# RWKV norm of a hybrid layer: scale, shift and bonus merged with the gate in the input projection, its rows reordered block by block

## The chip, the cores and the metric

The kernel runs on one core of a Trainium2 chip. The metric is the device time of one execution in microseconds. The engines of a core work side by side: TensorE (PE, with its weight loads PEld), VectorE (DVE), ScalarE (ACT), GpSimd (POOL) and SyncE (SP), which issues most DMAs.

## The reference, cut to what matters

One layer of a hybrid backbone: 2048 latent tokens and 256 context tokens, width 1024. One input projection feeds two groups of heads, a bidirectional RWKV-7 (512 wide, 8 heads of 64) and a latent attention (512 wide). Each is multiplied by its own SiLU gate; one output projection, the residual and a final norm follow.

```
u_sh, g_rw, u_mla, g_mla = split(h @ w_in)           # h: normed, modulated x
us = token_shift(u_sh, mu)                           # us + mu_prev*(prev-us) + mu_next*(next-us)
r, k, v, ... = split(us)                             # 512 channels each
y = y_f + y_b                                        # RWKV scans of both directions
yn = (y - mean) * rsqrt(var + 64e-5) * lnx_g + lnx_b # over the 64 channels of a head
bonus = sum(r * (k_dir[0] + k_dir[1]) * r_k, -1) * v # sum over a head, times v
rw_l = (yn + bonus) * silu(g_rw)
mla_l = attention(...) * silu(g_mla)
x = x + gate * (concat(rw_l, mla_l) @ w_out);  out = rms_norm(x) * final_g
```

## The kernel before, in words

**Projection.** `h` stands in SBUF with channels on the partitions, as a high and a low half. Two sweeps cover the tokens: the first 1026 latent ones with the 256 of the context, then the rest. In a sweep each *row* is a block of 128 columns of `w_in` (class `Row`): its weights are loaded into `wraw` by SP (L95, one buffer), split into `whi` on ACT and `wlo` on POOL, and multiplied with each group of tokens in 24 matmuls (L117: `whi` by high, `whi` by low, `wlo` by high, 8 each). A row has three latent groups of 342 columns (`h0`, `h1`, `h2`); rows with `ctx=True` have a fourth of 256 (`hc`) in the first sweep. ACT copies each result to `u` (four buffers). The next row's object, and with it the load of its weights, is made after the first group of the current row (`row`, L839).

Work behind a row is a generator in `self.pend`; `step` runs one step of the first of them after each sixth matmul, and `flush` runs all that are left. So the order in which rows are written sets under which rows the work of a block lies. The framework's scheduler decides the final order on each engine in this phase, from this order and from costs of its own.

**Order of rows in `sweep`.** First latent rows and the decay and rate rows, then for each of four blocks of 128 channels an `r` and a `k` row; then four `v` rows; then gate rows (six in the first sweep, eight in the second, where `ada_gate` adds two matmuls of a single row to each of the first four). After an `r`, `k` pair `flush` runs, `shift` (L848) makes the shifted `r` in `usr` (one buffer) and the shifted `k` in `us` (two buffers): one ACT pass and two DVE passes each. Then `rk_block` (L907) is queued, which lies under the next two rows: for each piece of at most 512 tokens `rk_piece` (L927) squares `k`, sums the squares over a head on PE with `blk`, a matrix with two blocks of ones (L937), multiplies decay and rate by their small weights (L954, L955), makes decays, directions and their running sums (POOL, ACT, DVE) and stores them to `s_x` (L969, L979). At its end it makes `bs = (kd0 + kd1) * r_k * r` (DVE, L988, which reads `usr`) and queues `finish`, run one piece later or by `last_bonus` (L921): four matmuls of two columns (L994) sum `bs` over each head, and DVE copies the sums to `bon`, one number for each token and head. `v_piece` (L1003) transposes the shifted `v` on PE and stores it to `s_v`, tokens on the partitions. `gate_out` (L815) makes `g = (tanh(u/2) + 1) * u / 2` and stores it to `s_g` on SP in the first sweep, on POOL or ACT in the second.

**Middle.** `qkv`, the RWKV chunks and the attention follow; PE's order there is written out by hand (`core`, L1190). An attention job takes scores in two passes: maxima first (L1307 on PE, `TENSOR_REDUCE` L1308 on DVE), then exponentials (L1427 to L1429 on PE, L1431 on ACT), accumulations on POOL (L1436) and values on PE (L1454).

**Tail.** Under the last four jobs (11 to 14 of the list) `late` (L1236) hands out, at each of its calls, a share of the steps of `post` (L1484), so that they are through after `POST_T` of the calls; the rest goes to `out_tiles`, the output projection (L1611). `post` loads the output weights, multiplies them by the gate, splits them, and then does 16 tiles of 128 tokens, three of which are under way at a time. On DVE a tile has: add of both directions (L1548), sum (L1551) and mean (L1553), subtraction (L1554), **bonus times `v`** (L1557), sum of squares (L1559, L1560), **plus shift** `lb` (L1567), times the inverse deviation (L1569), **times scale** `lg` (L1571), sum of both (L1573), product with the gate out of the transposed bank (L1582), and the low half of the split (L549). Each `yield` is one step.

## Time and profile before

| | |
|---|---|
| runs of the kernel before | median 2989.06 us, 2982.56 to 3002.37 us, 3 runs |
| the profiled execution | 3012.28 us, span of the trace 3010.5 us |
| PE (TensorE) | 2714.7 us busy, 90% of the span |
| PEld (weight loads) | 2061.7 us, 68% |
| DVE (VectorE) | 1810.0 us, 60% |
| POOL (GpSimd) | 1389.4 us, 46% |
| ACT (ScalarE) | 1285.2 us, 43% |
| HBM | 111 GB/s over the span |

Busy shares are averages over stages that have different limits, so a change is weighed in the stage in which it lies. The first stage (to about 190 us) makes the first `h`; the sweeps lie at 190 to 499 us and 641 to 946 us; `post` runs from 2428 to 2763 us; after that only output tiles and the last attention work are left. In rows of the trace "A <- B" reads "A waited for B", and a number behind an x counts instructions.

### The profile page before, as it was taken

The page shows a single profiled execution, that of the slowest core. Times are in us where ns is not written, and L with a number is a line of the kernel's source. Part 1 is how long each engine was busy: PE and PEld are TensorE (multiplying, and loading weights), DVE is VectorE, ACT ScalarE, POOL GpSimd, SP SyncE. Part 2 cuts the span into 40 slices and gives each one's busy share as a digit, 9 for nine tenths or more (in the row PEclk, how much of TensorE's full clock was granted, in tenths as well). Part 3 has the DMA queues.
Part 4 walks back from the last instruction along what each step waited for, and adds up shares of the span by engine and source line. Part 5 has one row for each costly group of instructions (what it writes and reads, how often), then busy time and mean ns, then how long its engine had stood idle before and what let it go on. Part 6 is the DMA issues. An engine that isn't in the chain of part 4 may idle for free.

```text
span 3010.5 us, 55075 instructions
## 1 busy us (share of the span) xinstructions
PE 2714.7 (90%) x22035; PEld 2061.7 (68%) x22035; DVE 1810.0 (60%) x2832; ACT 1285.2 (43%) x2245; POOL 1389.4 (46%) x1220
## 2 busy tenths in 40 slices
PE   5999999999998898999998999998999977888998
PEld 3997899987788787666666666566666644445776
DVE  3346843346623566777765777666677667997223
ACT  3446744446533432454443444444454432332221
POOL 2323322323332122566665666565566545776332
PEclk7998999999999998999998999999999977889999
DMA  5224552225554876222132222133122054343543
GB/s 200 82 87 124 136 161 92 80 92 140 149 157 160 267 224 162 75 86 70 54 103 82 61 71 69 52 101 99 58 76 61 22 153 117 110 126 108 150 134 119
DMA packets 409466, 336.66 MB, mean 112 GB/s; under 512 B 130598, under 2 KB 341841, under 8 KB 408185
## 3 DMA queue, kind: packets, MB, share of 16 engines
q1 hardware_dynamic: 405775, 327.19, 37.1%
q8 instruction: 173, 2.83, 0.4%
q0 software_dynamic: 992, 3.21, 0.3%
q10 hardware_dynamic: 2442, 2.73, 0.3%
q14 instruction: 84, 0.69, 0.1%
HBM read 210.68 MB, written 122.31 MB: 111 GB/s over the span
## 4 chain that ended last, share of the span: by engine, by line
PE 64%; DVE 15%; DMA 7%; ACT 5%; issue 4%; POOL 3%; SPq 1%; ACTq 0%; POOLq 0%; DVEq 0%
PE pm L117 18%; PE bo L1454 7%; PE bx L1611 6%; PE bs L1427 4%; DVE m L1308 3%; DMA x<-s_x 3%; PE bs L1429 3%; PE bs L1307 3%; PE bs L1428 3%; PE bx L331 3%; PE bs L1097 2%; ACT pt L1431 2%; PE bc L407 2%; DVE x L251 2%; PE bx L433 1%
## 5 line engine op out<-in xcount | busy, mean ns | idle before, releaser
L1436 POOL TENSOR_TENSOR acc<-acc,pt 128x512 f32<-128x512 f32 x512 | 662.6, 1308 | 581.3 <-ACT pt L1431 577.3
L1431 ACT ACTIVATE pt<-bs 128x512 f32<-128x512 f32 x576 | 342.7, 596 | 523.7 <-PE bs L1429 497.5
L1308 DVE TENSOR_REDUCE m<-bs 128x1 f32<-128x512 f32 (+1 forms) x736 | 400.0, 567 | 187.8 <-PE bs L1307 183.9
L1427 PE MATMUL bs<-q,kt 97*128 97x512 f32 x576 | 283.7, 493 | 46.5 <-DVE m L1308 27.9
L1454 PE MATMUL bo<-pt,vt 128*64 128x512 f32 x1152 | 301.8, 648 | 0.0
L549 POOL TENSOR_TENSOR wlo<-wraw,whi 128x1024 fp32r<-128x1024 f32 (+1 forms) x56 | 134.5, 2401 | 264.7 <-PE pm L117 163.9
L1307 PE MATMUL bs<-kt,q 96*128 96x512 f32 (+1 forms) x480 | 183.1, 410 | 71.1 <-ACT pt L1431 31.7
L1429 PE MATMUL bs<-q,kt 97*128 97x512 f32 x576 | 238.5, 414 | 0.0
L1428 PE MATMUL bs<-q,kt 97*128 97x512 f32 x576 | 238.1, 413 | 0.0
L1427 PEld LDWEIGHTS bs<-q,kt 97*128 97x128 f32 x576 | 113.5, 197 | 124.7 <-DVE m L1308 38.9
L1307 PEld LDWEIGHTS bs<-kt,q 96*128 96x128 f32 x480 | 91.5, 191 | 139.9 <-ACT pt L1431 68.2
L132 ACT COPY u<-pm 128x342 f32<-128x342 f32 (+1 forms) x168 | 73.9, 441 | 210.9 <-PE pm L117 209.5
L1454 PEld LDWEIGHTS bo<-pt,vt 128*64 128x64 f32 x1152 | 77.1, 146 | 121.1 <-issue 114.0
L1429 PEld LDWEIGHTS bs<-q,kt 97*128 97x128 f32 x576 | 114.9, 200 | 27.7
L1611 PE MATMUL bx<-wohi,big 128*128 128x512 f32 x496 | 126.0, 395 | 4.0 <-DMA big<-s_mix 4.0
L1428 PEld LDWEIGHTS bs<-q,kt 97*128 97x128 f32 x576 | 115.9, 201 | 4.8
L978 POOL TENSOR_TENSOR xt<-z,nk 128x512 f32<-128x512 f32 (+1 forms) x40 | 53.2, 1329 | 142.7 <-ACT z L977 82.0
L1611 PEld LDWEIGHTS bx<-wohi,big 128*128 128x128 f32 x496 | 93.7, 190 | 25.2 <-issue 4.9
L371 DVE TENSOR_TENSOR R<-bx,R 128x512 f16<-128x512 f32 x108 | 73.6, 682 | 59.1 <-PE bx L331 58.0
L1647 DVE TENSOR_TENSOR acc<-bx,big 128x512 f32<-128x512 f32 x32 | 22.1, 689 | 143.3 <-PE bx L1611 138.3
L826 DVE SCALAR_TENSOR_TENSOR kd<-z,u 128x512 f32<-128x512 f32 x32 | 38.9, 1218 | 111.4 <-ACT z L824 111.4
L348 DVE TENSOR_TENSOR bdg<-bx,lvl 64x512 f16<-64x512 f32 x144 | 98.6, 685 | 5.2 <-PE bx L331 2.6
(320 smaller groups left out, 6392.8 us busy)
## 6 DMA issues: line engine op xcount, KB each, us to landing
wraw<-in_w_in SPq DMA_DIRECT2D x54, 512.0 KB
x<-s_x SPq DMA_DIRECT2D x72, 384.0 KB
s_x<-xt SPq DMA_DIRECT2D x32, 512.0 KB
big<-s_mix SPq DMA_DIRECT2D x24, 512.0 KB
s_kn<-hl SPq DMA_DIRECT2D x36, 256.0 KB
ar<-s_nr SPq DMA_DIRECT2D x72, 128.0 KB
uv<-s_v SPq DMA_DIRECT2D x72, 128.0 KB
s_x<-cum SPq DMA_DIRECT2D x32, 256.0 KB
```

Source lines behind the costliest of these rows:

```text
L117: nc.tensor.matmul(ps[0:m, 0:w], a[:, k, 0:m], x[:, k], start=n == 0, stop=n == 3 * KT - 1)
L348: nc.vector.tensor_tensor(self.bd[name][ur, :, ur], x[ur], self.lvl[ur, i, ur].unsqueeze(1).to_broadcast([64, 8, 64]), op=ALU.mult)
L549: (eng_lo or nc.vector).tensor_tensor(lo, x, hi.bitcast(F32), op=ALU.subtract)
L1307: nc.tensor.matmul(ps[:, 0:w], q[0:96, e, 0, i * P:(i + 1) * P], ks[e], start=True, stop=True)
L1308: nc.vector.tensor_reduce(m5[:, e * NQS + i, j:j + 1], ps[:, 0:w], axis=AX.X, op=ALU.max)
L1427: nc.tensor.matmul(ps, ks[:, e, 0, sl], q[:, e, 0], start=True, stop=False)
L1428: nc.tensor.matmul(ps, ks[:, e, 0, sl], q[:, e, 1], start=False, stop=False)
L1429: nc.tensor.matmul(ps, ks[:, e, 1, sl], q[:, e, 0], start=False, stop=True)
L1431: nc.scalar.activation(pt, ps, AF.Exp, scale=SCALE)
L1436: nc.gpsimd.tensor_tensor(acc[e], held[e] if kt == 1 else acc[e], pt, op=ALU.add)
L1454: nc.tensor.matmul(oo[64 * e:64 * e + 64], VS[j][:, i, 64 * e:64 * e + 64], pts[kt, e], start=kt == 0, stop=kt == NK - 1)
L1611: nc.tensor.matmul(ps, x[:, i], a[:, k, 512 * h:512 * h + 512], start=n == 0, stop=n == last)
```

## The change

It does three things.

1. The rows of a sweep are ordered block by block: `v`, `r`, `k`, gate of block 0, then of block 1, and so on; the gate rows that belong to the attention come last, and `ada_gate` goes behind gate row 4. `rk_block` is queued after the `k` row and so lies under the gate row of its block and the `v` row of the next.
2. Shift, scale and bonus move into the projection, where channels are on the partitions. `bs` gets half of `r_k`; `finish` sums it with one matmul of 512 columns whose result has each head's sum on all of its 64 partitions, and multiplies the shifted `v` with it in place. The new `gate_rwkv(b)` runs after the `v` row of the next block: g = (tanh(u/2) + 1) * u, vp = (v * bonus/2 + lnx_b/2) * g, gl = g * lnx_g/2, and SP stores `vp` to the new `s_vb` and `gl` to `s_g`.
3. In the tail a tile is then y_normed (transposed) * gl + vp. The bonus product, the shift's add and the scale go; the remaining operations are spread over the steps anew. `POST_T` goes from 0.75 to 0.7, and the count of steps in `late` from 11 a tile to 7.

Cut to what matters:

```
     def sweep(...)
         for b in range(4):
-            specs += [(b * P, P, False), (512 + b * P, P, True)]
-        specs += [(1024 + b * P, P, True) for b in range(4)]
-        specs += gates[:6] if s == 0 else gates
+            specs += [(1024 + b * P, P, True), (b * P, P, False), (512 + b * P, P, True), gates[b]]
+        specs += gates[4:6] if s == 0 else gates[4:]
...
+        gg = None
         for b in range(4):
-            rr, kk = self.row(), self.row()
+            vv = self.row()
+            self.flush()
+            if b:
+                self.gate_rwkv(b - 1, gg, uv)
+            rr = self.row()
+            vs = self.shift(vv, 8 + b)
...
+                    self.pend.append(self.v_piece(b, c0 + o, us[:, o:o + n], n))
+            uv = vs[-1]
+            kk = self.row()
             self.flush()
             r = self.shift(rr, b, tag="usr")
...
-            self.pend.append(self.rk_block(b, pieces))
-        self.pend.append(self.last_bonus())
...
+            self.pend += [self.rk_block(b, pieces, uv), self.last_bonus()]
+            gg = self.row()
...
+    def gate_rwkv(self, b, rows, uv):
+        nc, up = self.nc, self.up
+        v0, v, _ = uv
+        for c0, u, i, w in rows:
+            for o in range(0, w, 512):
+                n = min(512, w - o)
+                uu = u[:, i + o:i + o + n]
+                th = up.tile([P, 512], F32, name="z")
+                nc.scalar.activation(th[:, 0:n], uu, AF.Tanh, scale=0.5)
+                g = up.tile([P, 512], F32, name="kd", bufs=3)
+                nc.vector.scalar_tensor_tensor(g[:, 0:n], th[:, 0:n], 1.0, uu, op0=ALU.add, op1=ALU.mult)
+                vp = v[:, c0 - v0 + o:c0 - v0 + o + n]
+                nc.vector.scalar_tensor_tensor(vp, vp, self.hln[:, 4 + b:5 + b], g[:, 0:n], op0=ALU.add, op1=ALU.mult)
+                gl = up.tile([P, 512], F32, name="kd", bufs=3)
+                nc.scalar.activation(gl[:, 0:n], g[:, 0:n], AF.Identity, scale=self.hln[:, b:b + 1])
+                t0 = c0 + o - self.CT
+                nc.sync.dma_start(self.s_vb[b][:, t0:t0 + n], vp)
+                nc.sync.dma_start(self.s_g[b][:, t0:t0 + n], gl[:, 0:n])
...
         def finish():
             ps = self.pq.tile([P, 512], F32, name="pq")
-            nt = n // P
-            for j in range(nt):
-                nc.tensor.matmul(ps[:, 2 * j:2 * j + 2], bs[:, j * P:(j + 1) * P], self.blk[:, 0:128:64],
-                                 start=True, stop=True)
-            t0 = (c0 - self.CT) // P
-            nc.vector.tensor_copy(self.bon[:, t0:t0 + nt, 2 * b:2 * b + 2],
-                                  ps[:, 0:2 * nt].rearrange("p (j h) -> p j h", h=2))
+            nc.tensor.matmul(ps[:, 0:n], self.blk, bs, start=True, stop=True)
+            vp = uv[1][:, c0 - uv[0]:c0 - uv[0] + n]
+            nc.vector.tensor_tensor(vp, vp, ps[:, 0:n], op=ALU.mult)
...
     def late(self, rest):
-        self.pc += (34 + 11 * (L // P)) / (self.POST_T * rest)
+        self.pc += (34 + 7 * (L // P)) / (self.POST_T * rest)
...
-    POST_T = 0.75
+    POST_T = 0.7
...
     def post(...)
-                V.tensor_tensor(vt, vt, bc(self.bon[:, tt], 64), op=ALU.mult)
-                yield 1
...
+                mx = b_ya[:, 1]
+                V.tensor_tensor(mx, ps, b_vg[:, 0], op=ALU.mult)
...
-                V.tensor_tensor(flat(vt), flat(vt), lb, op=ALU.add)
-                yield 1
-                V.tensor_tensor(y, y, bc(st[:, 0], 64), op=ALU.mult)
-                yield 1
-                V.tensor_tensor(flat(y), flat(y), lg, op=ALU.mult)
-                yield 1
-                V.tensor_tensor(y, y, vt, op=ALU.add)
...
-                V.tensor_tensor(mx, ps, vg[:, 1], op=ALU.mult)
+                V.tensor_tensor(mx, mx, b_vg[:, 1], op=ALU.add)
```

**PE, second block of the first sweep.** These rows are PE's instructions where the `rk` work of block 1 begins, in the kernel before. `h0h` and `h0l` are the halves of the first group of tokens, `blk` is the matrix that sums over heads, L937 the sum of squares; the row of the projection that runs here is `r` of block 2.

```order
L117 MATMUL pm<-h0h,whi 128x342 x8
L117 MATMUL pm<-h0l,whi 128x342 x8
L117 MATMUL pm<-h0h,wlo 128x342 x4
L937 MATMUL pq<-sq,blk 128x256
L117 MATMUL pm<-h0h,wlo 128x342 x4
L117 MATMUL pm<-h1h,whi 128x342 x8
L117 MATMUL pm<-h1l,whi 128x342 x7
L937 MATMUL pq<-sq,blk 128x512
L954 MATMUL pq<-lx_1126,lwh_1122 128x256
L955 MATMUL pq<-lx_1126,lwl_1115 128x256
```

And in the changed kernel, where L937 has become L971 and L954, L955 have become L988, L989; the row of the projection here is the gate row of block 1.

```order
L117 MATMUL pm<-h0h,whi 128x342 x8
L117 MATMUL pm<-h0l,whi 128x342 x8
L117 MATMUL pm<-h0h,wlo 128x342 x2
L971 MATMUL pq<-sq,blk 128x256
L117 MATMUL pm<-h0h,wlo 128x342 x6
L117 MATMUL pm<-h1h,whi 128x342 x8
L117 MATMUL pm<-h1l,whi 128x342 x2
L971 MATMUL pq<-sq,blk 128x512
L988 MATMUL pq<-lx_1130,lwh_1126 128x256
L989 MATMUL pq<-lx_1130,lwl_1119 128x256
```

The first sum of squares stands four matmuls into `h0h,wlo` before and two now; the second, and the decay weights behind it, five matmuls earlier than before. The row beneath has no shift and no `rk` work of its own to come.

**SP, first sweep.** These are SP's DMAs around a gate row in the kernel before: `wraw` is the load of a row's weights, `s_g` a store of a gate piece.

```order
L1014 DMA s_v<-sq 128x4x128
L584 DMA us<-in_x 114x1024
L1014 DMA s_v<-sq 128x4x128
L833 DMA s_g<-kd 128x512
L95 DMA wraw<-in_w_in 128x8x128
L833 DMA s_g<-kd 128x512 x2
```

In the changed kernel SP has the following at the end of block 0, where `s_x` are the last stores of its `rk` work, and L866, L867 the stores of `gate_rwkv`.

```order
L1003 DMA s_x<-cum 128x8x64
L1013 DMA s_x<-xt 128x8x128
L866 DMA s_vb<-us 128x512
L867 DMA s_g<-kd 128x512
L866 DMA s_vb<-us 128x512
L867 DMA s_g<-kd 128x512
L95 DMA wraw<-in_w_in 128x8x128 x2
```

Four stores of `gate_rwkv` now stand in a row ahead of two loads of weights; before, one gate row's two stores stood between two loads.

**DVE, in the tail.** These are DVE's instructions for about one tile of `post` before; `acc` holds `v` and the gate, `big` the outputs of both directions, `bx` the transposed bank.

```order
L1551 TENSOR_REDUCE st<-big 128x8
L1557 TENSOR_TENSOR acc<-acc,bon 128x512
L1553 TENSOR_SCALAR st<-st 128x8
L1567 TENSOR_TENSOR acc<-acc,lb 128x512
L1554 TENSOR_TENSOR big<-big,st 128x512
L1569 TENSOR_TENSOR big<-big,st 128x512
L1557 TENSOR_TENSOR acc<-acc,bon 128x512
L1559 TENSOR_REDUCE st<-big 128x8
L1571 TENSOR_TENSOR big<-big,lg 128x512
L1560 TENSOR_SCALAR st<-st 128x8
L1582 TENSOR_TENSOR big<-bx,acc 128x512
L1573 TENSOR_TENSOR big<-big,acc 128x512
```

And now, where L1571 is the add of both directions, L1577 the subtraction, L1608 the product with the inverse deviation, L1587 the product with the gate, L1598 the add of `vp`, and L554 the low half of the split.

```order
L1571 TENSOR_TENSOR big<-big 128x512
L1574 TENSOR_REDUCE st<-big 128x8
L1575 TENSOR_SCALAR st<-st 128x8
L1577 TENSOR_TENSOR big<-big,st 128x512
L1590 TENSOR_REDUCE st<-big 128x8
L1591 TENSOR_SCALAR st<-st 128x8
L1608 TENSOR_TENSOR big<-big,st 128x512
L1335 TENSOR_REDUCE m_28660<-bs 128x1
L1587 TENSOR_TENSOR big<-bx,acc 128x512
L1598 TENSOR_TENSOR big<-big,acc 128x512
L554 TENSOR_TENSOR big<-big 128x512
```

The products with `bon` and `lg` and the add of `lb` are gone, and the product with the gate comes ahead of the one add that is left; a row of the maxima (L1335, L1308 before) stands among them.

## Rows read from the trace of the kernel before

**Rows 1.** The page's 40 slices: busy tenths of PE and of DVE.

```profile
PE   5999999999998898999998999998999977888998
DVE  3346843346623566777765777666677667997223
```

**Rows 2.** By stage: us, PE, PEld, DVE, ACT, POOL busy (instructions), PE clock, DMA, GB/s.

```profile
2428.00:2483.00 55.00, 39.70 (x114) 22.37 (x115) 41.79 (x70) 19.01 (x32) 21.24 (x17) 0.69 0.55 155
2483.00:2763.00 280.00, 224.31 (x786) 120.32 (x785) 250.82 (x363) 91.14 (x159) 198.35 (x141) 0.85 0.39 113
2763.00:3010.50 247.50, 236.76 (x1012) 175.69 (x1012) 60.41 (x88) 47.44 (x83) 72.04 (x64) 0.98 0.45 136
...
2550.00:2650.00 100.00, 82.48 (x305) 43.83 (x305) 93.53 (x132) 35.05 (x62) 76.13 (x54) 0.90 0.40 119
2650.00:2763.00 113.00, 90.12 (x331) 48.40 (x328) 105.92 (x147) 38.16 (x67) 84.87 (x60) 0.91 0.37 105
```

**Rows 3.** Waits, 2428 to 2763: waiter <- releaser, total us, times, longest us.

```profile
PE bs L1427 <- DVE m L1308: 22.2, 15, 4.9
...
PE bs L1307 <- DVE m L1308: 13.4, 12, 5.7
```

**Rows 4.** Busy time by pairs or groups of rows of the projection (columns as Rows 2).

```profile
215.30:255.30 40.00, 38.71 (x208) 31.60 (x207) 29.95 (x28) 30.09 (x50) 12.88 (x8) 1.00 0.47 124
255.30:306.90 51.60, 46.75 (x217) 37.60 (x216) 30.77 (x33) 31.78 (x52) 14.31 (x10) 0.83 0.43 110
306.90:349.50 42.60, 39.58 (x215) 32.55 (x214) 34.19 (x32) 30.71 (x49) 14.78 (x9) 1.00 0.49 131
349.50:391.50 42.00, 42.00 (x239) 35.40 (x239) 35.92 (x41) 34.14 (x55) 15.61 (x10) 1.00 0.57 148
...
429.50:498.80 69.30, 69.30 (x445) 69.25 (x444) 21.78 (x30) 23.78 (x40) 14.41 (x6) 1.00 0.36 112
...
663.90:698.90 35.00, 32.64 (x174) 26.87 (x172) 21.81 (x19) 22.90 (x34) 13.12 (x8) 1.00 0.41 106
...
734.20:773.40 39.20, 35.24 (x182) 28.28 (x182) 27.58 (x25) 24.65 (x37) 12.50 (x8) 0.96 0.53 137
...
842.80:945.70 102.90, 101.07 (x617) 92.10 (x616) 29.97 (x39) 28.80 (x49) 29.37 (x25) 1.00 0.38 117
```

**Rows 5.** Waits of ACT and of PE, 200 to 860 us (columns as Rows 3).

```profile
ACT usr L855 <- DVE sq L988: 17.1, 6, 3.9
...
PE pq L937 <- ACT sq L934: 14.9, 9, 3.6
```

**Rows 6.** Groups on DVE, 2480 to 2763: busy us, mean ns | idle before, releaser.

```profile
L1308 DVE TENSOR_REDUCE m<-bs 128x1 f32<-128x512 f32 x96 | 63.3, 679 | 7.1 <-PE bs L1307 6.4
...
L1571 DVE TENSOR_TENSOR big<-big,lg 128x512 f32<-128x512 f32 x16 | 16.9, 1056 | 0.1
...
L1557 DVE TENSOR_TENSOR acc<-acc,bon 128x512 f32<-128x512 f32 x16 | 15.6, 978 | 1.3 <-DMA acc<-s_v 1.3
...
L1567 DVE TENSOR_TENSOR acc<-acc,lb 128x512 f32<-128x512 f32 x16 | 14.9, 934 | 0.0
```

**Rows 7.** Line L1557: shortest, median and longest in ns; first and last start.

```profile
L1557 DVE TENSOR_TENSOR acc<-acc,bon x16: 676/680/1815, 2487.0 to 2729.8; 128x512 f32<-128x512 f32 x16
```

**Rows 8.** Groups on PE and DVE, 90 to 930 us (columns as Rows 6).

```profile
L937 PE MATMUL pq<-sq,blk 128*128 128x512 f32 x32 | 20.9, 764 | 14.9 <-ACT sq L934 14.9
...
L994 PE MATMUL pq<-blk,sq 128*128 128x2 f32 x128 | 16.5, 251 | 9.4 <-DVE sq L988 7.3 <-ACT xt L974 2.2
...
L826 DVE SCALAR_TENSOR_TENSOR kd<-z,u 128x512 f32<-128x512 f32 x28 | 36.1, 1293 | 97.1 <-ACT z L824 97.1
```

**Rows 9.** Timeline of SP: start us, us, queue, line and transfer.

```profile
444.70 0.37 SPq L95 DMA_DIRECT2D wraw<-in_w_in  x1
...
456.07 0.38 SPq L95 DMA_DIRECT2D wraw<-in_w_in  x1
...
261.24 0.36 SPq L979 DMA_DIRECT2D s_x<-xt  x1
```

More of the change, by code (lines that the diff above doesn't have):

```diff
@@ L768, in sweep @@
                     pieces.append((c0 + o, us[:, o:o + n], r[0][1][:, o:o + n] if c0 >= self.CT else None, n))
-            self.pend.append(self.rk_block(b, pieces))
-        self.pend.append(self.last_bonus())
-        for b in range(4):
-            rows = self.row()
-            self.flush()
-            first = True
-            for c0, us, w in self.shift(rows, 8 + b):
-                for o in range(0, w, 512):
-                    n = min(512, w - o)
-                    self.pend.append(self.v_piece(b, c0 + o, us[:, o:o + n], n, first))
-                    first = False
-        if s == 0:
-            for b in range(6):
-                self.gate_out(b, self.row())
+            self.pend += [self.rk_block(b, pieces, uv), self.last_bonus()]
+            gg = self.row()
+        if s == 0:
+            for b in range(4, 6):
+                rows = self.row()
+                if b == 4:
+                    self.flush()
+                    self.gate_rwkv(3, gg, uv)
+                self.gate_out(b, rows)
             self.flush()
@@ L786, in sweep @@
         pg = self.pt.tile([P, 512], F32, name="pp")
-        for b in range(8):
-            if b < 4:
-                self.pend += [self.ada_gate(2 * b, pg), self.ada_gate(2 * b + 1, pg)]
-            self.gate_out(b, self.row())
+        for b in range(4, 8):
+            rows = self.row()
+            if b == 4:
+                self.flush()
+                self.gate_rwkv(3, gg, uv)
+            self.pend += [self.ada_gate(2 * b - 8, pg), self.ada_gate(2 * b - 7, pg)]
+            self.gate_out(b, rows)
         self.flush()
@@ L905, in norm_store, with rk_block @@
                 yield 1
-    def rk_block(self, b, pieces):
+    def rk_block(self, b, pieces, uv):
         bonus = self.bonus
         for i in range(0, len(pieces), 2):
-            pair = [self.rk_piece(b, *p, bonus) for p in pieces[i:i + 2]]
+            pair = [self.rk_piece(b, *p, bonus, uv) for p in pieces[i:i + 2]]
             for _ in range(2):
@@ L1512, in load @@
             nc.sync.dma_start(ya, self.s_y[:, a0:a0 + P].rearrange("d p c -> p d c"))
-            nc.sync.dma_start(vg[:, 0], self.s_v[a0:a0 + P])
-            nc.sync.dma_start(vg[:, 1].rearrange("p (b t) -> p b t", t=P),
-                              self.s_g[0:4, :, t0:t0 + P].rearrange("b p t -> p b t"))
+            for i, s_ in enumerate((self.s_g, self.s_vb)):
+                nc.sync.dma_start(vg[:, i].rearrange("p (b t) -> p b t", t=P),
+                                  s_[0:4, :, t0:t0 + P].rearrange("b p t -> p b t"))
             return ya, vg
```

53 lines of the change are left out of this document (28 added, 25 removed).

## The prediction

> **What bounds the kernel now.** I read the page's slices first, then busy time by stage, then for each stage the waits. The slices [rows 1] show PE at 9 tenths nearly everywhere, so a change off PE is worth something only where PE falls short. The longest such place is the stretch before the output projection (slices 33 to 37), where PE drops to 7 and 8 and DVE stands at 7 to 9. In the projection (slices 3 to 13) the slices are too coarse; there I go by single rows, below.
>
> In the stage table [rows 2] the norm of the RWKV output (`post`) is the stretch from 2428 us on: first the output weights (to 2483), then the sixteen tiles (to 2763, 280.0 us). In the tiles DVE is busy for 250.8 us, 90%, PE for 224.3 at a granted clock of 0.85, POOL for 198.4. In the last 113 us DVE reaches 105.9, 94% [rows 2]. PE's largest waits there are for DVE's maxima [rows 3], which queue behind the tile work on DVE. So DVE sets the pace of these tiles. Behind them, from 2763, PE is busy for 236.8 of 247.5 us: the end is bound by PE.
>
> In the projection PE runs one row (72 matmuls of 342 columns) after another: six gate rows take 69.3 us [rows 4], 11.55 each, with nothing in the way. A row with the 256 context columns costs 24 x 256/342 matmuls more, 2.9 us (estimate). Two rows that carry a `rk_block` take more than that: in the first sweep 40.0 us, then 51.6, 42.6 and 42.0; in the second 35.0 first, 39.2 later [rows 4]. The first pair of either sweep is the shortest. What the later ones add is in the waits [rows 5]: the shift of the next r row on ACT waits for DVE's bonus product of the block before (17.1 us in 6 waits, one `usr` buffer), and PE then waits for the square that ACT makes behind it (14.9 us in 9 waits).
>
> **The tail: what is removed.** Per tile three DVE operations of 128x512 go: the bonus product (L1557, 15.6 us for 16), the shift's add (L1567, 14.9) and the scale (L1571, 16.9) [rows 6], together 47.4 us. The gate product from PSUM and one add stay. The lost loads of scale and shift and the swap of `s_v` for `s_vb` leave as many loads per tile as before. Upper bound of the gain: DVE falls to 203.4 us and keeps its share of 90%, so 227 us for 280, 53 less. Lower bound: the same operation takes 676 to 680 ns when undisturbed and up to 1815 ns [rows 7]; 48 x 0.68 is 32.6, and if it counts only in the stretch from 2550 where DVE has no slack (213 of 280 us) it is 25. I take 40: 47.4 x 213/280 is 36, and 4 for the first tiles, where DVE still has slack. POOL's 198.4 us come close under the new 203.4, which is why I don't take 53.
>
> Here a rule of the Trainium skill speaks against the larger figure. The stretched durations are seen in the minimum and maximum of L1557 [rows 7]. The page GPSIMD Engine Reference, section Key points, says that GpSimd shares its SBUF interfaces with VectorE and that this contends with instructions with two SBUF inputs, which all three removed operations are. By that rule the stretch belongs to POOL's accumulations and moves to whichever operation remains: the tail would give 32.6 and not 47.4 us of DVE time.
>
> **The tail: the pace.** `late` hands out post's steps. Before: 34+11x16 = 210 steps over 0.75 of 225 calls, 1.24 a call. Now the formula has 34+7x16 = 146 over 0.7, 0.93 a call, but a tile has eight yields, so 161 steps take 174 calls where 168 did: one macro step of attention (5 calls) moves from the PE-bound end into the DVE-bound stretch. That is about 3 us more of maxima there (L1308: 63.3 us over 28 macro steps, 2.3 each [rows 6]) and as much PE time less behind it; it cancels. The output steps then run at 2.14 a call, not 2.66, so some 45 of them come after the attention's end. PE is full there either way [rows 2], so the order costs nothing; without that cover the last job's finishing chain would show, under 10 us (estimate). Sum for the tail: -40.
>
> **The projection: what moves.** Rows go v, r, k, gate for each block, and `rk_block(b)` now runs under gate row b and v row b+1. As the order shows, PE's first `rk` matmul of every block then stands where it stood in the first block before, and the r shift that uses the one `usr` buffer comes two rows later, so the wait of [rows 5] has nothing left to wait for. I price every pair as the first one. First sweep, from the end of the rows r0, k0 (215.3) to 498.8, 283.5 us now: three pairs at 40.0 and one of two gate rows at 37.1 make 157.1; v0, three r, three k and one gate row are 4 x 11.55 + 4 x 14.4 = 104; 40 transposes of v at 0.12 (estimate from 342 columns at 0.16, two passes) 4.8; sum 266. Second sweep, 663.9 to 945.7, 281.8 us now: 4 x 35.0 + 7 x 11.55 + the last three gate rows with all of `ada_gate` (102.9 - 5 x 11.55 = 45.2) + 3.8 = 270.
>
> Added on PE: the bonus sum is one fp32 matmul of 512 columns per piece where it was four of two columns. [rows 8] list 764 ns x 32 records for the like matmul (two records a piece) against 251 x 128 (eight a piece); the records overlap. From below 0 (they take turns on the same array), from above 2 x 0.76 = 1.5; I take 0.3, as the two differ little in PE's busy time (20.9 us over 16 like pieces against 16.5 over 16). 16 x 0.3 = 5. Added on DVE: per piece a second product of 1.3 us (as L826, [rows 8]) and one from PSUM, 16 pieces, at most 32 us over both sweeps. They hide in the r and k rows, which carry no `rk` work: DVE is busy 21.8 of 69.3 us in the gate rows, which are their like [rows 4]. Without that cover they would cost those 32 us. ACT takes the scaling by g instead; same cover.
>
> A wait that is new: on SP the next weights (`wraw`) stand behind the four stores of `s_vb` and `s_g`, which wait for the block's last bonus. In the gate rows one load leaves every 11.37 us [rows 9], one per row; the row of the load at 444.7 begins five such rows before 498.8, at 442.0, so a load leaves 2.7 us after its row begins, the next row starts in time, and it lands within 8.7. Of the first pair the last store of the block left at 261.24 [rows 9], 6 us into the row that begins at 255.3. With the gate products after it I expect the stores at 7 to 8 us, and 2 us of stall in the four blocks of the first sweep: 8. In the second the bonus lies ahead of the row's end: 0. Sum: 266+8 = 274 and 270, with 5 for the bonus 549 against 565.3: -16. Bounds: -35 (no pair stalls at all beyond half of now) and 0.
>
> **The sum.** The profiled execution took 3012.3 us, 23 above the median of the runs (2989.1), so I carry the difference over: -40 - 16 = -56, 2956 for an execution like the profiled one, 2933 for the median.
>
> **Rivals.** (1) The stretch moves on: removed operations are worth 0.68 us each and the tail gives 25. For it the bimodal 676 to 1815 ns; against it that POOL is idle for 82 of the 280 us. -25 - 16: 2948. (2) Something else takes over the tail: PE at a low clock or POOL. For it PE's clock of 0.69 in the weights and POOL's 198 us; against it the waits of [rows 3], which name DVE. The tail gives 10, the projection 10: 2969. (3) Slower: weights behind stores. If a load lands 8.7 us after its issue and the split takes 1 us more, PE stalls by x - 1.8 us per block, x being the time into the r row at which the stores leave. All gains (56) and 1% (30) are eaten when 8 (x - 1.8) passes 86, x above 12.6, later than the row is long. At x = 15 it is 8 x 13.2 = 106, so 3039. For it: the order of SP; against it the 6 us of [rows 9].
>
> **How the numbers follow.** Forecast 0.62 (own range 2910 to 2955), rival 1 0.14, rival 2 0.17, rival 3 0.07. From 2905 (tail -47, projection -35, rounded) up to 2975, which takes in rivals 1 and 2, leaves out rival 3 and the ends, under 2 in 10. A run of this kernel tells about 1% (30 us): faster than 2959 holds the forecast and rival 1, less their upper ends, 0.74; within 1% rival 2 and those ends, 0.19; slower 0.07.
>
> **What would show it.** Right: DVE's share in the tile stretch falls below 85% and the stretch is 235 to 250 us; PE's waits for the maxima shrink; pairs of gate and v row take 40 and 35 us, and no `usr` wait for the bonus remains. Wrong: the removed operations' neighbours grow longer than 1.05 us (rival 1); PE waits for ACT's exponentials or POOL instead (rival 2); PE stands at the start of k rows while POOL splits weights that came late (rival 3).

## The result, and the profile after

The changed kernel takes 3015.2 us in the median of 20 runs, the kernel before 2995.8 in 20 runs: the ratio is 1.006, with an interval of 1.0040 to 1.0079. It is slower by 19 us where 56 less were forecast. The profiled execution of the changed kernel took 3007.1 us, 8 below its median, and that of before 3012.3 us, 16 above its own, so the two traces alone show no difference; a second trace of each (runs before2 and after2 below) is read beside them.

A measure that holds across kernels is needed. Attention has 16 jobs of 9 macro steps (18 key tiles in pairs), 144 in all; a macro step is four score products of PE (L1427 before, L1454 after), so step n (from 0) begins with the (4n+1)th of them. I cut each trace at step 0, 101 (about where the work of `post` begins), 105, 133 and the end. Steps 105 to 132, 28 of them, carry all but the edges of the tiles' work in both kernels.

| part, us | before, before2 | after, after2 |
|---|---|---|
| between the sweeps (end of the first sweep's rows to the second's first full row) | 61.3, 60.1 | 72.7, 72.0 |
| start to macro step 0 | 1195, 1184 | 1196, 1196 |
| step 0 to 101 | 1241, 1231 | 1239, 1240 |
| 101 to 105, output weights | 57, 54 | 47, 50 |
| 105 to 133, the tiles | 276, 274 | 274, 275 |
| 133 to the end | 243, 243 | 249, 248 |

What steps 101 to 105 gain, 6.5 us on average, is lost behind step 133, 6 us.

Busy time in the parts that the change touches, after, in the columns of [rows 2]:

```profile
494.60:567.30 72.70, 58.57 (x362) 55.19 (x361) 31.40 (x71) 36.51 (x65) 24.93 (x26) 0.93 0.34 109
...
2482.00:2756.00 274.00, 222.47 (x769) 122.91 (x767) 203.39 (x301) 88.98 (x154) 184.89 (x137) 0.84 0.38 109
2756.00:3005.00 249.00, 235.49 (x1010) 176.10 (x1008) 65.37 (x93) 49.54 (x85) 72.04 (x65) 0.98 0.47 141
```

And before, cut at the same steps:

```profile
498.80:560.10 61.30, 56.95 (x361) 55.69 (x361) 33.20 (x71) 35.55 (x65) 25.45 (x26) 0.92 0.23 70
...
2492.00:2768.00 276.00, 221.50 (x780) 119.30 (x778) 243.11 (x348) 88.72 (x155) 194.01 (x137) 0.86 0.39 115
2768.00:3010.00 242.00, 231.91 (x998) 173.23 (x998) 60.41 (x88) 47.44 (x83) 72.04 (x64) 0.99 0.44 132
```

DVE did lose its work among the tiles, 243.1 to 203.4 us, 88% to 74%. The stretch did not follow: 276 to 274 us. DVE stands idle 38 us longer, and 20 of these are one wait, first before, then after (columns as in [rows 3]):

```profile
DVE big L1569 <- POOL st L1566: 4.9, 4, 1.5
```
```profile
DVE big L1608 <- POOL st L1592: 24.6, 12, 4.0
```

The product with the inverse deviation now waits 24.6 us for the power -1/2, a small operation on POOL. Two of these waits in the timeline of DVE, and POOL's power of the first, after:

```profile
2637.95 0.55 DVE L1591 TENSOR_SCALAR st<-st 128x8 f32<-128x8 f32 x1
...
2640.64 1.75 DVE L1608 TENSOR_TENSOR big<-big,st 128x512 f32<-128x512 f32 x1 [0.94 <-POOL st L1592]
...
2656.30 0.16 DVE L1591 TENSOR_SCALAR st<-st 128x8 f32<-128x8 f32 x1
2658.21 1.74 DVE L1608 TENSOR_TENSOR big<-big,st 128x512 f32<-128x512 f32 x1 [1.76 <-POOL st L1592]
...
2638.58 2.02 POOL L1592 TENSOR_TENSOR st<-st,mhalf 128x8 f32<-128x8 f32 x1
```

L1591 ends the variance, POOL takes 2.02 us for its power, and DVE starts L1608 at its end. Before, the product of a tile stood far behind its second statistic; the last of what stood between for one tile:

```profile
2605.06 1.06 DVE L1557 TENSOR_TENSOR acc<-acc,bon 128x512 f32<-128x512 f32 x1
2606.05 0.16 DVE L1553 TENSOR_SCALAR st<-st 128x8 f32<-128x8 f32 x1
2606.12 0.68 DVE L1567 TENSOR_TENSOR acc<-acc,lb 128x512 f32<-128x512 f32 x1
2606.72 0.68 DVE L1554 TENSOR_TENSOR big<-big,st 128x512 f32<-128x512 f32 x1
2607.33 1.77 DVE L1569 TENSOR_TENSOR big<-big,st 128x512 f32<-128x512 f32 x1
```

In the trace of before DVE has seven or more other instructions between L1560 and L1569 in 12 of the 16 tiles, work of the next tile and maxima for the most part. In the changed kernel it has none between L1591 and L1608 in nine tiles.

What stands behind L1608 on DVE waits too, the maxima among it. In the same steps PE still waits for maxima, 21.4 us in 16 waits, where it was 25.4 in 21 before. Against these 4 us stand the three waits for the next jobs' queries (`q`), 18.4 us where it was 13.2. First before, then after:

```profile
PE bs L1427 <- DVE m L1308: 18.5, 12, 4.9
PE bs L1307 <- DMA q<-s_qr: 13.2, 3, 5.5
PE bs L1307 <- DVE m L1308: 6.9, 9, 3.1
```
```profile
PE bs L1334 <- DMA q<-s_qr: 18.4, 3, 7.0
PE bs L1334 <- DVE m L1335: 12.1, 10, 2.3
PE bs L1454 <- DVE m L1335: 9.3, 6, 2.9
```

In the projection ACT's wait for the bonus product [rows 5] is gone, and the pairs of rows that carry the `rk` work take what the first pair took before, or less ([rows 4]: 40.0 and 35.0). The second block of the first sweep and the first of the second:

```profile
299.00:338.90 39.90, 38.58 (x201) 31.01 (x200) 31.50 (x30) 30.87 (x50) 13.21 (x9) 1.00 0.46 122
671.00:703.20 32.20, 31.65 (x172) 26.59 (x171) 17.04 (x15) 17.71 (x26) 6.11 (x3) 1.00 0.35 87
```

What they gave is lost between the sweeps: this stretch takes 59.9 to 61.3 us in all seven traces here with the old order of rows and 70.2 to 75.8 in all thirteen with the new one. Timelines of SP and PE there, after:

```profile
492.62 4.83 SPq L847 DMA_DIRECT2D s_g<-kd  x3
497.51 1.44 SPq L589 DMA_DIRECT2D xt<-in_x  x3
...
507.19 0.45 PE L656 MATMUL pp<-ident,xt 114*128 114x114 f32 x1 [3.42 <-DVE xt L595]
```

The second sweep's inputs leave SP at 497.5 us, behind the last gate stores and after the last row (494.6). Before, they had left under the last v and the first gate rows, 60 to 87 us ahead of the sweep's end at 498.8:

```profile
412.23 1.20 SPq L584 DMA_DIRECT2D xt<-in_x  x2
...
438.38 0.29 SPq L584 DMA_DIRECT2D us<-in_x  x1
```

Behind the second sweep there is a smaller seam: the middle's first matmul stands 5.8 us behind the last row (5.6 in after2), where it was 0.5 in both traces of before, and waits for its first load:

```profile
954.75 1.44 PE L1124 MATMUL bs<-c,khi 128*128 128x256 f32 x4 [3.94 <-DMA c<-s_c]
```

### The profile page after: what moved, and what is told of

Same layout as the page of the kernel before. It is cut to its first block, busy times and chain, and to the rows that moved or that the text cites. A ratio compares the mean times of both kernels' runs of the same rounds, so it can differ in the third digit from the quotient of the medians.

```text
span 3005.2 us, 54842 instructions
## 1 busy us (share of the span) xinstructions
PE 2699.3 (90%) x21939; PEld 2045.4 (68%) x21939; DVE 1777.1 (59%) x2786; ACT 1296.1 (43%) x2261; POOL 1381.4 (46%) x1212
## 4 chain that ended last, share of the span: by engine, by line
PE 43%; DVE 11%; DMA 7%; ACT 4%; issue 2%; POOL 1%; SPq 1%; ACTq 0%; POOLq 0%; DVEq 0%
PE bo L1481 7%; PE bx L1631 5%; PE bs L1454 4%; DVE m L1335 3%; DMA x<-s_x 3%; PE bs L1456 3%; PE bs L1334 3%; PE bs L1455 3%; PE bx L331 3%; ACT pt L1458 2%; PE bc L407 2%; PE bs L1124 2%; DVE x L251 2%; PE bx L433 1%; PE pm L117 1%
## 5 line engine op out<-in xcount | busy, mean ns | idle before, releaser
L1335 DVE TENSOR_REDUCE m<-bs 128x1 f32<-128x512 f32 (+1 forms) x736 | 400.1, 568 | 180.1 <-PE bs L1334 176.5
L1454 PE MATMUL bs<-q,kt 97*128 97x512 f32 x576 | 283.6, 492 | 38.6 <-ACT pt L1458 20.1
L554 POOL TENSOR_TENSOR wlo<-wraw,whi 128x1024 fp32r<-128x1024 f32 (+1 forms) x56 | 134.6, 2404 | 311.3 <-PE pm L117 164.6
L1454 PEld LDWEIGHTS bs<-q,kt 97*128 97x128 f32 x576 | 113.6, 197 | 115.7 <-ACT pt L1458 39.1
L1667 DVE TENSOR_TENSOR acc<-bx,big 128x512 f32<-128x512 f32 x32 | 22.0, 692 | 151.9 <-PE bx L1631 140.9
L331 PEld LDWEIGHTS <-bdg 128*128 128x128 f16 x1728 | 67.7, 99 | 44.8 <-issue 42.2
```

The lines of the kernel that those rows point to most:

```text
L331: nc.tensor.matmul(ps[:, h], lhsT[:, h], r, start=plus is None, stop=also is None and (plus is None or h == 7))
L554: (eng_lo or nc.vector).tensor_tensor(lo, x, hi.bitcast(F32), op=ALU.subtract)
L1335: nc.vector.tensor_reduce(m5[:, e * NQS + i, j:j + 1], ps[:, 0:w], axis=AX.X, op=ALU.max)
L1454: nc.tensor.matmul(ps, ks[:, e, 0, sl], q[:, e, 0], start=True, stop=False)
```

## The experiments: the tail

**b_relief** takes the three operations out of the kernel before.

```
-                V.tensor_tensor(vt, vt, bc(self.bon[:, tt], 64), op=ALU.mult)
...
-                V.tensor_tensor(flat(vt), flat(vt), lb, op=ALU.add)
...
-                V.tensor_tensor(flat(y), flat(y), lg, op=ALU.mult)
```


> The kernel before, with the three DVE operations of each tile (bonus product, add of the shift, product with the scale) left out and nothing else changed: order of rows, steps and their pace stay, so bonus, shift and scale are missing from the output. Theory A (DVE sets the pace of the tiles, as predicted): the tile stretch goes from 280 to 240 to 255 us, the whole is 25 to 40 us shorter, ratio 0.987 to 0.992. Theory B (a tile step waits for its place among the attention's macro steps of about 10 us each, and DVE counts only by the 35.6 us in which PE waits for maxima): DVE's share in the tiles falls to 75%, the stretch stays at 268 to 280 us, ratio 0.996 to 1.001.

Measured: 1.0032 (1.0001 to 1.0062). Steps 105 to 133 in its trace, and DVE's largest wait in them:

```profile
2480.00:2758.00 278.00, 217.29 (x779) 117.77 (x777) 209.80 (x303) 89.48 (x156) 188.24 (x137) 0.86 0.40 116
```
```profile
DVE big L1567 <- POOL st L1565: 25.2, 14, 5.4
```

DVE lost 33 us of work and got 20 more of this wait: at most three instructions now stand between L1559, the second statistic, and L1567, its product, in 14 of the 16 tiles. Theory A, the forecast's, falls: nothing of the projection or of the pace is changed here, and the tiles gain nothing. Theory B had the stretch right, but not the cause (b_notile).

**b_relief_recip** is b_relief with this power replaced by a DVE reciprocal:

```
-                nc.gpsimd.tensor_tensor(st[:, 0], st[:, 1], self.mhalf.to_broadcast([P, 8]), op=ALU.pow)
+                V.reciprocal(st[:, 0], st[:, 1])
```


> As b_relief (three DVE operations of each tile left out), and the power -1/2 of the variance, a small POOL operation that DVE then waits for, replaced by a DVE reciprocal of the same 8 columns, so the deviation's root is left out too. Theory H (DVE stands 25 us behind POOL's power in b_relief, the maxima stand behind it, and this took back what the three operations gave): the stretch of the tiles goes from 275 to 250 to 262 us, ratio 0.993 to 0.998. Rival (what a tile costs lies in PE's order and clock, not in this wait): the stretch stays at 270 us or more, ratio 1.000 to 1.005.

Measured: 0.9927 (0.9900 to 0.9954), 0.0105 below b_relief, and 255 us for the 28 steps:

```profile
2482.00:2737.00 255.00, 215.72 (x780) 116.06 (x779) 202.16 (x315) 89.50 (x155) 159.41 (x121) 0.89 0.43 126
```

PE's waits for the maxima behind DVE's product go with the wait: 25.9 us in b_relief, 10.7 here.

```profile
PE bs L1307 <- DVE m L1308: 18.8, 13, 4.9
PE bs L1427 <- DVE m L1308: 7.1, 6, 2.9
```
```profile
PE bs L1307 <- DVE m L1308: 6.1, 10, 1.0
PE bs L1427 <- DVE m L1308: 4.6, 8, 1.1
```

**a_recip** makes the same replacement in the changed kernel.

> The changed kernel with the power -1/2 of the variance replaced by a DVE reciprocal of the same 8 columns (the root is left out), nothing else. Theory H: DVE loses its 24.6 us of waiting for POOL's power in the tiles, as b_relief_recip did, and the tail is 18 to 25 us shorter than the changed kernel's, ratio to before 0.997 to 1.001. Rival (the changed order of steps has a bound of its own): tail within 8 us of the changed kernel's, ratio 1.003 to 1.008.

Measured: 0.9968 (0.9939 to 0.9996) against 1.006 for the changed kernel; 28 steps in 243 us, 31 less than after. Both lose POOL's 28 to 30 us of powers as well, so these two don't tell the wait from POOL's load. The next one does.

**a_poolmul_only** keeps the power on POOL and moves the product behind it, so that no DVE operation waits for it:

```
-                V.tensor_tensor(y_, y_, bc(st_[:, 0], 64), op=ALU.mult)
+                nc.gpsimd.tensor_tensor(y_, y_, bc(st_[:, 0], 64), op=ALU.mult)
```


> The changed kernel with the product with the inverse deviation on POOL, and nothing else. Tail 546 to 550 us where the changed kernel has 566 to 570, front as in the changed kernel (1196 to 1200 us to the first exponential, 72 to 73 us between the sweeps): ratio to before 0.998 to 1.001, that is 0.006 below the changed kernel. If the gain of a_poolmul came with its other edits: tail 560 us or more, ratio 1.003 or more.

Measured: 1.0003 (0.9983 to 1.0024). POOL has 204 us of work in these steps instead of 185, and they take 247 us:

```profile
2488.00:2735.00 247.00, 208.88 (x768) 114.00 (x769) 191.78 (x285) 88.79 (x154) 204.00 (x153) 0.90 0.42 121
```

PE's waits for maxima fall from 21.4 to 9.5 us (5.3 and 4.2). POOL's load is not the cost: it rises, and the stretch falls. But DVE lost 16 products here too, so this run bounds the wait together with them. The gain repeats: in all five traces with this move in the changed kernel the time from step 101 to the end is 546 to 553 us, in five without it (after, after2, a_xq, a_xq2, a_xq_ada) 569 to 576.

Of the 27 us of the stretch, 14 are PE's own: its busy time falls from 222.5 to 208.9 us for the same matmuls, and the mean granted clock is 0.90 of full speed instead of 0.84 (0.82 over the 292 us of b_poolmul, 0.94 over the 218 of b_notile, both below). So the stretch gains more than the time in which PE stands still; why the clock moves with it is not shown.

**b_poolmul** makes the same move in the kernel before, where the next operation on DVE, the scale, needs the product.

> The kernel before with the product with the inverse deviation on POOL, nothing else. Theory H: DVE waits only 5 us for POOL's power there, so all that can be had is the operation itself, 16 x 1.1 us of DVE's work, worth 0.5 us each as in b_double: 5 to 10 us, ratio 0.996 to 0.999; the merge is then worth the rest of a_poolmul's 22 us in the tail. Rival (the product on POOL gives the same in either kernel): tail 546 to 552 us, ratio 0.991 to 0.994, and the merge is worth nothing.

Measured: 1.0058 (1.0027 to 1.0090), outside what either theory gave. DVE loses 10 us of work, gains a wait, and the stretch grows by 16 us:

```profile
2477.00:2769.00 292.00, 227.88 (x781) 122.05 (x780) 233.38 (x332) 88.56 (x155) 210.56 (x153) 0.82 0.38 111
```
```profile
DVE big L1571 <- POOL big L1569: 20.0, 6, 5.1
```

My expectation had overlooked that scale. It is the mechanism from the other side: a DVE operation that stands behind a POOL result costs more than its own time. It also says what the merge can give: with the scale gone from behind the product, POOL can take the product at a gain; with the scale there it was a loss.

**b_notile** leaves all operations of the tiles out of the kernel before; loads, steps and stores stay.

> The kernel before with no tile work in post at all: the loads, the steps and the stores stay, every operation of the sixteen tiles is left out (the loaded values are stored unnormed). Theory B1 (the attention's own macro step of about 10 us paces the stretch): the stretch of the tiles stays at 262 to 276 us, ratio 0.995 to 1.000. Theory B2 (a macro step costs 6.8 us, which is its PE work, and each tile adds 5.3 us by its chain of engines, whatever of DVE's work is taken out of it): the stretch falls to 28 x 6.8 = 190 to 210 us, 65 to 85 us less, ratio 0.972 to 0.980.

Measured: 0.9809 (0.9743 to 0.9874, four runs); 28 steps in 218 us, 7.8 each:

```profile
2484.00:2702.00 218.00, 191.82 (x714) 103.54 (x715) 89.12 (x147) 72.82 (x124) 147.88 (x121) 0.94 0.49 151
```

So the operations of all sixteen tiles cost 58 us (276 less 218), not the 280 of the stretch; neither theory had it exactly, B2 (65 to 85 less) was nearer.

**b_double** adds three more operations of the same kind to each tile of the kernel before.

> The kernel before with three DVE operations of 128x512 more in each tile (the shift added twice more and taken off once, the scale multiplied twice, so the output has a wrong scale and shift). DVE's work in the tiles goes from 249 to 283 us (48 x 0.7) or 297 (48 x 1.0), above the stretch of 276. Theory F (the three operations of the change lay in idle time and waits, the next three don't): the stretch grows by 25 to 45 us, ratio 1.008 to 1.015. Theory A as predicted (DVE had 10% left and each operation counts): the same, 35 to 50 us. Rival (DVE's operations are hidden on this side too): under 10 us, ratio under 1.004.

Measured: 1.0091 (1.0060 to 1.0121); the stretch 300 us, 24 more, 0.5 for each operation, with DVE 91% busy. That is the lower edge of theory F. The price of an operation is not symmetric here: 48 more cost 24 us, 48 fewer gave none.

```profile
2482.00:2782.00 300.00, 238.24 (x781) 121.62 (x780) 273.65 (x396) 89.06 (x155) 203.04 (x137) 0.83 0.37 106
```

**a_pace60** hands the tiles out faster (`POST_T = 0.6`, `34 + 8 * (L // P)` steps).

> The changed kernel with the count of steps per tile put to the 8 that it has and POST_T at 0.6: 162 steps over 135 calls of late instead of 161 over 174, so the tiles are done in about 27 macro steps of attention instead of 35, and 8 macro steps move under the output projection. Theory B: each moved macro step costs about 10 us among the tiles and its PE work of about 7 us under the output projection, so 8 x 3 = 24 us less than the changed kernel, ratio to before 0.997 to 1.000. Theory A: DVE's 212 us of work, less 8 x 2.3 of maxima, in a stretch of about 211 us is full again, and the kernel stays within 8 us of the changed one, ratio 1.003 to 1.009.

Measured: 1.0030 (0.9995 to 1.0066). From the first tile's add to the last one's it takes 230 us where the changed kernel takes 284, and from there to the end 300 instead of 242. The 8 moved macro steps cost 6.7 to 7.3 us on either side: theory B's 10 us is wrong, and the pace is worth nothing measurable.

## The experiments: the projection

**b_order** has the new order of rows and nothing else of the change.

```
-            specs += [(b * P, P, False), (512 + b * P, P, True)]
-        specs += [(1024 + b * P, P, True) for b in range(4)]
+            specs += [(1024 + b * P, P, True), (b * P, P, False), (512 + b * P, P, True), gates[b]]
...
```

Where the expectations of b_order, a_xq and a_xq_ada speak of 142 or 153 us, they count the stretch between the sweeps up to the end of the second sweep's first rows (142.3 us before, 153.7 after).

> The kernel before with the order of rows of the changed one (v, r, k, gate by block, ada_gate behind gate row 4) and nothing else: bonus, gates and tail as before. Theory C (the new order ends the block work at the very end of a sweep, where the second sweep's first loads and the middle's first loads have no cover): the first sweep is some 3 to 10 us shorter, the stretch from the end of the first sweep to the end of the second sweep's first rows is about 10 us longer (153 instead of 142), and the whole is within 0.998 to 1.005. Rival (the merged gate with its products and stores is what costs in the projection, the order alone saves): both sweeps shorter by 8 us each, no longer stretch between them, ratio 0.992 to 0.996.

Measured: 1.0043 (1.0007 to 1.0079); 70.2 us between the sweeps, and macro step 0 at 1209 us, 14 to 24 later than in the two traces of before. The stretch comes with the order, and the order alone costs: the rival falls. That the first sweep would be shorter was wrong: it ends at 505.0 us instead of 498.8.

**a_xq, a_xq_ada, a_xq2** try to take the stretch back. a_xq:

```
-                nc.sync.dma_start(xt[0:tw], src[...])
+                (nc.gpsimd if t0 else nc.sync).dma_start(xt[0:tw], src[...])
```


> The changed kernel with the input loads of the second sweep issued from POOL's queue, so that they don't stand behind the last gate rows' stores on SP. Theory C1 (it is the queue): the loads leave some 10 us earlier, the stretch between the sweeps goes from 153.7 to 142 to 146 us, ratio to before 1.002 to 1.004 where the changed kernel has 1.006. Theory C2 (the loads wait for buffers that the last block's work holds, whatever the queue): the stretch stays at 150 us or more, ratio 1.005 to 1.008.

Measured: 1.0020 (0.9986 to 1.0054), but 72.4 us between the sweeps: the ratio lies where C1 had it, the stretch does not, and the stretch decides. A load into `us` stood on POOL 10.9 us for the last store out of that buffer, and POOL's own norm work behind it.

a_xq_ada also puts `ada_gate` under the r and k rows.

> The changed kernel with the second sweep's input loads on POOL's queue and ada_gate put back under the r and k rows, so that nothing but gate rows is left at the sweep's end. Theory C1: the stretch between the sweeps 142 to 149 us, the middle's first matmuls at most 2 us behind the last row instead of 6; the latter is given back by 1200 us, as the two first profiles show, so 8 to 14 us less than the changed kernel, ratio 1.001 to 1.003. Rival (the handoff behind the second sweep is worth its 7 us in full): ratio 0.998 to 1.000.

Measured: 1.0014 (0.9982 to 1.0045), 73.5 us between the sweeps. The middle's first matmul is back at 0.5 us behind the last row, so it was `ada_gate` that held it, but the last row itself ends no earlier (948.8, after 948.7 and 943.8). a_xq2 moves only the loads into `xt` (`nc.gpsimd if t0 and not place else nc.sync`).

> The changed kernel with only those loads of the second sweep's input on POOL's queue that go to the xt buffers (three of the first six); those to us and usr stay on SP. Theory C1 (SP's order costs the 12 us): the three loads leave by 491 us instead of 497.5, nothing on POOL stands behind a load that waits, the stretch from the end of the first sweep's rows to the second sweep's first full row goes from 72.5 to 61 to 66 us, ratio to before 1.001 to 1.003. Theory C2 (us is held until the last stores of s_vb, and these loads pace it): 70 us or more, ratio 1.004 to 1.007.

Measured: 1.0080 (1.0048 to 1.0111), 75.8 us: the stretch grew, so theory C1 falls here too.

**a_us3_xq_poolmul** gives `us` a third buffer, so that all these loads can leave early.

> The changed kernel with a third us buffer (paid for by one uc and one usc buffer less), all input loads of the second sweep on POOL's queue, and the product with the inverse deviation on POOL. Theory C3 (buffer and queue together held the loads): the six loads of the second sweep's first two groups leave by 493 us, PE's stall there goes, the stretch between the sweeps 60 to 65 us (72.5 in the changed kernel, 60.1 before), tail 546 to 550 us, ratio 0.990 to 0.994. Rival (the norm, the transposes and the last block's work meet at the sweep's end whatever the loads do): the stretch stays at 69 us or more, ratio 0.995 to 1.000.

Measured: 0.9987 (0.9965 to 1.0008), 73.4 us between the sweeps. The loads do leave early, from POOL, and a third link shows on DVE:

```profile
488.25 0.52 POOL L589 DMA_DIRECT2D us<-in_x  x1
...
489.41 0.52 POOL L589 DMA_DIRECT2D usr<-in_x  x1
```
```profile
498.44 0.69 DVE L840 SCALAR_TENSOR_TENSOR kd<-z,u 128x512 f32<-128x512 f32 x1 [6.32 <-DMA s_g<-kd]
...
502.08 0.15 DVE L593 TENSOR_SCALAR ss<-ss 114x1 f32<-114x1 f32 x1
```

The last gate products wait for `kd` buffers whose stores are under way, and the norm of the new inputs (L593) stands behind them. Theory C3 falls: queue and buffers of the loads don't suffice. What is left, argued and not shown, is that block 3's products, the last gates and the next sweep's inputs now meet at the sweep's end. That a row or two of cover there would end it was not tried.

**a_poolmul, a_poolmul2, a_xq2_poolmul.** a_poolmul is a_xq_ada with the product on POOL; a_poolmul2 is the same once more; a_xq2_poolmul sets it on a_xq2. The expectations follow in the order a_poolmul, a_xq2_poolmul, a_poolmul2.

> As a_xq_ada, with the product of a tile with its inverse deviation moved from DVE to POOL, behind POOL's own power, so that DVE never waits for it. Theory H: DVE loses another 20 us of work and 25 us of waiting in the tiles, PE's waits for maxima fall from 22 to under 12 us, and the stretch of the tiles goes from 284 to 262 to 274 us, ratio 0.994 to 0.999. Rival (POOL is the next bound: 16 products of 1.4 to 2 us more on 188 of 284 us, ahead of the accumulations): the stretch stays at 280 us or more, ratio 1.000 to 1.004.

> a_xq2 with the product of a tile with its inverse deviation on POOL. If both remedies add up: the tail 546 to 550 us as in a_poolmul (566 to 570 in the changed kernel), the front 6 to 10 us shorter than in the changed kernel, ratio to before 0.990 to 0.995. If a_poolmul's gain came from its front (1187 us to the first exponential in its trace): 0.996 to 1.001.

> a_poolmul once more, to see whether its ratio of 0.995 holds: 0.993 to 0.998 if the tail's 20 us are worth what they seem, 0.998 to 1.001 if the first figure was low by chance, as the spread between a_xq, a_xq_ada and a_xq2 (1.002, 1.001, 1.008) lets one think.

Measured: a_poolmul 0.9949 (0.9918 to 0.9980), a_xq2_poolmul 1.0000 (0.9975 to 1.0025) and a_poolmul2 0.9975 (0.9960 to 0.9990). The 28 steps take 254, 251 and 251 us, so all three have the gain in the tail; what a_xq2_poolmul lacks lies ahead of it (step 0 at 1207 us, after 1187 and 1199). a_poolmul is a version that beats both kernels, by 0.25 to 0.5% against before; of its two figures 0.9975, from 12 runs after 10, is the safer one.

**before2, after2** are second traces.

> The kernel before once more, for a second trace: the first trace is 10 to 15 us above the median of the runs, that of the changed kernel 8 us below its own, so the pair of traces shows no difference where the medians differ by 15 to 20 us. Theory V (the spread lies in the middle, from the first exponential to the first output weights, where both kernels have the same instructions on PE): the parts up to the first exponential (1191 to 1196 us) and from the output weights on (570 to 572 us) come out within 4 us of the first trace and the middle moves by up to 15 us. Rival (the tail itself varies): the tail moves by more than 8 us.

> The changed kernel once more, for a second trace, against before2. Theory V: up to the first exponential 1194 to 1200 us, the tail 563 to 570 us, so the part that the change touches gives nothing and costs nothing beyond 5 us; the middle differs between any two traces by up to 15 us. Rival: the projection or the tail of the changed kernel is 10 us or more longer than before2's.

Measured: 2987.5 and 3011.4 us; their parts are in the first table. Theory V is half right: the tails repeat, but the part up to macro step 0 moves by 11 us in the kernel before as well, so the 12 us by which after2's is longer than before2's tell nothing alone. Over all traces whose kernels have one of the two fronts unchanged, macro step 0 lies at 1184 to 1196 us in seven of the front of before (mean 1190) and at 1195 to 1200 in five of the changed one (mean 1196); steps 0 to 101 take 1235 against 1242 on average. The means of the front's parts, over the same traces (the first block row begins at 190 us in both):

| part, us | front of before (7) | changed front (5) |
|---|---|---|
| first sweep, from its first block row on | 308.5 | 305.1 |
| from there to the second sweep's first block row | 140.9 | 152.9 |
| second sweep, from there on | 306.9 | 299.8 |
| from its last row to macro step 0 | 243.5 | 248.9 |

## Why the prediction was wrong

**What failed first: "So DVE sets the pace of these tiles", and with it the -40.** The share of 90 to 94% was right, the conclusion was not. Before, POOL's 2 us for a tile's power passed under other work of DVE: seven or more instructions stood between the second statistic and the product in 12 of 16 tiles, and the bonus product or the shift's add stood there in as many. With the three operations out, the order of those that are left changed too, and the product came to stand right behind its statistic (none between in nine tiles). The wait grew from 4.9 to 24.6 us, and the stretch gained 0 to 2 us. b_relief, which keeps the steps as they were, shows the same. The forecast put nothing down for a wait on POOL's answer, though the rows of the changed order show it: L1590, L1591 and L1608 follow each other there, and L1608 needs POOL's power of what L1591 gives. Rival 2 was the nearest for the tail (10 us forecast, 1 measured) but had the wrong cause in POOL's load; a_poolmul_only raises that load and gains.

**The bounds.** 25 to 53 us for the tail were worked out from durations alone. Leaving a wait out of the lower bound made it too high: it had to reach to 0. The operations of all tiles together cost 58 us (b_notile), so the upper bound asked for nearly all of them.

**The rule on GpSimd and VectorE** (the Trainium skill, GPSIMD Engine Reference, Key points) was borne out in size: DVE's work fell by 33 us in b_relief, not 47.4, near the 32.6 by that rule. What remained grew: the product with the inverse deviation took 1096 ns before, 1497 in b_relief and 1263 in the changed kernel. The trace of before leans to POOL as the cause and doesn't prove it: POOL was busy for 91% of the time of the tile's 28 long two-input operations (over 1.6 us) and for 47% of that of the 80 short ones (under 0.72). It changed nothing in the time of the kernel.

**The pace.** That the macro step moved out of the end cancels was right, and a_pace60 shows it for 8 steps. That the output steps behind the attention cost nothing fits too: the tail from step 101 takes 575 and 570 us before, 570 and 573 after.

**The projection, -16.** The pairs were priced right: 39.9 for 40.0, 32.2 for 35.0. The transposes cost what the sum gave them: eight add 0.85 us to a k row of the second sweep, 0.11 each for 0.12. By the means of the front's parts the sweeps gave 3.4 and 7.1 us, 10.5 of the 16. A part of the rest is the sum of the bonus: over the projection PE stood 23.7 us in front of it (L1027), where it was 9.4 (L994, [rows 8]).

```profile
L1027 PE MATMUL pq<-sq,blk 128*128 128x512 f32 x32 | 18.6, 664 | 23.7 <-DVE sq L1022 17.3 <-ACT xt L1008 6.4
```

What the sum left out is the seam: it ended each sweep at its last row and asked nowhere who starts behind it. There the new order cost 12 us between the sweeps and 5 behind the second, by the same means. SP's queue was looked at, for the weights alone.

**Rival 3** (weights behind stores) did not come true. A block of the first sweep does lose 3 to 4.5 us in the first group of the next r row (24 matmuls in 6.7 and 8.3 us instead of 3.8), where 2 were forecast, but what PE waits for there is DVE's operand of the bonus sum (1.8 us each time), not weights.

**The signs.** DVE's share fell to 74%, the pairs took 40 and 32 us and the `usr` wait went, three of the signs named for being right, in a kernel that got slower. They told of work that moves, not of time; the stretch of 235 to 250 us was the one that told.

**What stays open.** Front and seam account for +6.6 us by the mean of traces, the tail for -1.1. The middle, whose instructions on PE are the same, is 7.6 us longer on average over five and seven traces, which spread by 18 and 11 us; whether this is the change's or chance is not settled, nor are the last 6 us to the measured 19. In the tail two experiments would tell more and were not run: the kernel before with all three operations and the power on DVE, and the changed kernel with the product set some instructions later on DVE. So it isn't shown how much of the 23 us of b_relief_recip belongs to the removed operations and how much would have come without the change.

## What to carry to other kernels

Before an operation is priced as gain, read the new order of its engine for an instruction that needs another engine's result: count what stands between the two before and after. If the work between is gone, the wait comes back, and only moving the waiting operation as well makes the removal a gain. A busy share says nothing on this; a run without the work altogether (here 58 us for sixteen tiles) gives a measure of what can be had. And where work is moved to the end of a stage, the next stage's first loads, their buffers and their place in the queues belong into the sum.

## What the runs showed of the hardware

48 two-input operations of 128x512 on DVE were worth 24 us when added (b_double), and 48 of the same kind nothing when removed (b_relief). Most of these operations, with both inputs in SBUF, took 0.68 to 0.69 us or 1.74 to 1.82, four of 32 between (L1557 [rows 7]; L1608); when POOL lost its powers (a_recip), L1608 fell from 1263 to 867 ns on average. POOL's power of 128x8 took 1.64 to 2.03 us (L1592, after), a DVE reciprocal of the same tile 0.20 (a_recip).
